# Late projection groups of a hybrid encoder layer: low weight parts from a copy in PSUM, token-major evictions through another ring

## The chip, the cores and the metric

The kernel runs on one core of a Trainium2 chip. The time is the device time of one execution in microseconds (us), the median of three runs. A separate execution was recorded by the hardware profiler, and all rows below come from that one. The engines are PE (TensorE), DVE (VectorE), ACT (ScalarE), POOL (GpSimd) and SP (SyncE, which here only issues DMAs). Each runs its own instruction stream strictly in the order in which it was built, and waits on semaphores.

## The reference

One layer on 512 tokens of width 2048. What matters here is the token mixing: one projection, whose columns feed four mixers.

```python
h = rms_norm(x, mix_pre_g) * (1.0 + sc_m) + sh_m
(a_q, a_k, a_v, a_gate, a_beta, a_alpha, b_q, b_k, b_v,
 c_q, c_k, c_v, d_u, d_v) = split(h @ w_in, offsets)
out_a = gated_deltanet(a_q, a_k, a_v, a_gate, a_beta, a_alpha, ...)   # conv, l2 norm, chunked delta rule
out_b = chunked_relbias_attention(b_q, b_k, b_v, rel_bias)            # 4 heads, softmax
out_c = swa_sink_attention(c_q, c_k, c_v, sinks, slopes)              # 4 heads, softmax
out_d = spatial_gating(d_u, d_v, sgu_norm_g, sgu_w, sgu_b)
y = concatenate([out_a, out_b, out_c, out_d]) @ w_out
x = x + gt_m * rms_norm(y, mix_post_g)
x = x + gt_f * rms_norm(conv_glu_ffn(...), ffn_post_g)                # the larger part of the time
```

The gates and shifts come from a matrix-vector product of `silu(c)` with `ada_w` (2048 x 12288), called the gemv below.

## The kernel before

Every large matmul is done in three passes on numbers split into a high and a low part (fp32r): `hi*hh + lo*hh + hi*hl`. A weight unit is a 128x1024 tile, loaded by one DMA into a ring `raw` (4 buffers) or, every second unit, into the ring `ada` (5), which the gemv's units use too. `wunit` cuts it into two halves of 128x512 and calls `split` for each. Without `shadow`, `split` writes `hi` on ACT and then `lo = raw - hi` on DVE. With `shadow`, ACT rounds the weights a second time into a PSUM tile `sh`, and DVE computes `lo = raw - sh` from that:

```python
        if shadow:
            sh = pp.tile([P, 512], F32R, tag=mtag(), name=nm("sh"), bufs=2)[:, :src.shape[1]]
            S.activation(sh, src, AF.Copy)
            S.activation(hi, src, AF.Copy)
            V.tensor_tensor(lo, src, sh, ALU.subtract)
            return
        S.activation(hi, src, AF.Copy)
        (eng or V).tensor_tensor(lo, src, hi, ALU.subtract)
```

PSUM holds two rings of 128x512 tiles. The ring `acc` (4 banks) holds the sums of the projections. The other (`mxa` and `mxb`, 2 banks each, taken in turn by `mtag()`) serves all tiles made by `mx(...)`: every matmul result of the DeltaNet, of the spatial gating and of the attentions. `sh` tiles come from that second ring. A ring hands its buffers out in the order in which the tiles stand in the program text: a tile gets its buffer when the tile that had it before has been read for the last time.

The input projection is done in groups. Early groups (step 0 to 5) run while the rows of `h` are being made. Late groups (`step is None`) are `bv`, `bk`, `ck`, `dv`, `bq`, `cq` and `du`: 52 weight units of 24 matmuls each, 1248 matmuls of 512 columns. `dv` and `bv` are token-major (`tm_group`), the rest feature-major (`fm_group`). Their results go through `ev_late_tm` (tiles `lt`) or `ev_late_fm` (`lf`) to DRAM. `between()` lets one to three background steps of the gemv in per unit (`RATE`).

In the program text the whole DeltaNet (lines 784 to 1046: convolutions and norms, decay matrices, a 32-step triangular solve on DVE at lines 944 and 946, and a recurrence of eight steps, lines 995 to 1046) comes first, then the groups `bv` to `dv`, the spatial gating, `bq`, the four heads of the `b` attention (lines 1096 to 1130), `cq`, `du`, the `c` attention (from line 1150) and the output projection. A scheduler then decides the order of each engine's stream: it may move an instruction ahead of others in the text as soon as its operands and its buffers are to be had.

Of the kernel before, what the change touches and what calls it, by code (L numbers as in the profile page):

```python
# [249 lines left out]
def trunk_kernel(ctx: ExitStack, tc: tile.TileContext, a: dict, out: bass.AP):  # L250
# [26 lines left out]
    def nm(s):  # L277
        uid[0] += 1
        return f"{s}{uid[0]}"

    def mt(s="m", shape=(P, 512), dt=F32):
        return cur[0].tile(list(shape), dt, tag="m", name=nm(s))

    def tt_(s="t"):
        return tp.tile([P, 512], F32, tag="t", name=nm(s))
# [4 lines left out]
    def acc(s="acc"):  # L290
        return pp.tile([P, 512], F32, tag="acc", name=nm(s))
# [56 lines left out]
    def wunit(src, nk, w, own=True, shadow=False):  # L348

        raw = wraw() if own else araw()  # L350
        nc.sync.dma_start(out=raw[:, :nk * w], in_=src[:, :nk * w])
        step = max(1, 512 // w)
        out_ = []
        for j in range(0, nk, step):
            m = min(step, nk - j) * w
            hi = wp.tile([P, 512], F32R, tag="hi", name=nm("hi"))
            lo = wp.tile([P, 512], F32R, tag="lo", name=nm("lo"))
            split(raw[:, j * w:j * w + m], hi[:, :m], lo[:, :m], None, shadow)
            out_ += [(hi[:, i * w:(i + 1) * w], lo[:, i * w:(i + 1) * w]) for i in range(min(step, nk - j))]
        return out_  # L360

    def wraw():
        return wp.tile([P, UW], F32, tag="raw", name=nm("raw"), bufs=NRAW)

    def araw():
        return gp.tile([P, UW], F32, tag="ada", name=nm("ada"), bufs=NADA)

    def split(src, hi, lo, eng=None, shadow=False):
# [10 lines that stand above are left out]
    def mm3(o, sh, sl, mh, ml, first, last):  # L379
        TE.matmul(o, sh, mh, start=first, stop=False)  # L380
        TE.matmul(o, sh, ml, start=False, stop=False)  # L381
        TE.matmul(o, sl, mh, start=False, stop=last)  # L382
# [156 lines left out]
    def between():  # L539
        pace[1] += pace[0]  # L540
        while pace[1] >= 1:
            pace[1] -= 1
            bg_step()

    def fm_group(g, evict, ws=None):
        _, keys, ks, step, us = g
        n = len(keys)
        if len(us) == 1:
            (ui, (uk, uc)) = us[0]
            if ws is None:  # L550
                ws = wunit(a["w_in"][ui], len(uk), len(uc), True, SH_IN and step > 0)
            for t in range(n):
                p_ = acc()
                o = slice(t * P, (t + 1) * P)
                for j, kt in enumerate(uk):
                    mm3(p_, ws[j][0][:, o], ws[j][1][:, o], hh[kt], hl[kt], j == 0, j == len(uk) - 1)
                evict(keys[t], p_, step)
            return
        ps = None
        for n_, (ui, (uk, uc)) in enumerate(us):  # L560
            ws = wunit(a["w_in"][ui], len(uk), len(uc), n_ % 2 == 0)
            between()
            if ps is None:
                ps = [acc() for t in range(n)]
            for j, kt in enumerate(uk):
                for t in range(n):
                    o = slice(t * P, (t + 1) * P)
                    mm3(ps[t], ws[j][0][:, o], ws[j][1][:, o], hh[kt], hl[kt], kt == ks[0], kt == ks[-1])
        for t in range(n):
            evict(keys[t], ps[t], step)  # L570

    def tm_mm(p_, sh, sl, wh, wl, first, last):
        TE.matmul(p_, sh, wh, start=first, stop=False)  # L573
        TE.matmul(p_, sh, wl, start=False, stop=False)  # L574
        TE.matmul(p_, sl, wh, start=False, stop=last)  # L575

    def tm_group(g, evict):
        _, key, ks, step, us = g
        ps = None
        for n_, (ui, (uk, uc)) in enumerate(us):  # L580
            w = len(uc)
            ws = wunit(a["w_in"][ui], len(uk), w, n_ % 2 == 0)
            between()
            if ps is None:
                ps = [acc() for _ in range(NTT)]
            order = [(j, tt) for j in range(len(uk)) for tt in range(NTT)]
            if len(us) == 1:
                order = [(j, tt) for tt in range(NTT) for j in range(len(uk))]
            for j, tt in order:
                kt = uk[j]  # L590
                sl = slice(tt * P, (tt + 1) * P)
                tm_mm(ps[tt][:, :w], hh[kt][:, sl], hl[kt][:, sl], ws[j][0], ws[j][1], kt == ks[0], kt == ks[-1])
        for tt in range(NTT):
            evict(key, tt, ps[tt], step)
# [62 lines left out]
    for s, ks in enumerate(KSTEPS):  # L657
        gs = [g for g in early if g[3] == s]
        fs = []
        upto = (KSTEPS[s + 1][-1] + 1) // 2 if s + 1 < len(KSTEPS) else 8  # L660
        while nextc < upto:
            fs += list(mod_units(nextc))
            nextc += 1
        for i, g in enumerate(gs):
            if s == 0 and i < 2:
                pass
            elif g[0] == "FM":
                fm_group(g, ev_early_fm)
            else:
                tm_group(g, ev_early_tm)  # L670
            n = -(-len(fs) // max(1, len(gs) - 2 - i)) if s else FS0[i]
            for f in fs[:n]:
                f()
            fs = fs[n:]
# [19 lines left out]
    def rtile(s, dt=F32):  # L694
        if mixing_open[0]:
            return gp.tile([P, 512], dt, tag="xn", name=nm(s), bufs=NBR)
        return mt(s, dt=dt)
# [62 lines left out]
        nc.sync.dma_start(out=std[STG[n_] + j], in_=t)  # L760

    def ev_late_tm(key, tt, ps, step):
        t = tt_("lt")
        S.activation(t, ps, AF.Gelu_apprx_tanh if key == "dv" else AF.Copy)  # L764
        nc.sync.dma_start(out=std[STG[key] + tt], in_=t)

    def late_groups(name, rate):
        pace[0] = rate
        for g in late:
            if (g[1][0][0] if g[0] == "FM" else g[1]) == name:  # L770
                if g[0] == "FM":
                    fm_group(g, ev_late_fm)
                else:
                    tm_group(g, ev_late_tm)

    def staged(name, j):
        t = mt("sd")
        nc.sync.dma_start(out=t, in_=std[STG[name] + j])
        return t
# [83 lines left out]
    for tt in range(NTT):  # L863
# [4 lines left out]
        t = mt("kp")  # L868
# [4 lines left out]
    for tt in range(NTT):  # L873
# [3 lines left out]
        t = mt("vt")  # L877
# [196 lines left out]
    for tt in range(NTT):  # L1074
        t = staged("dv", tt)
# [5 lines left out]
    for tt in range(NTT):  # L1081
        t = tmt[("dv", tt)]
        V.tensor_scalar(t, t, mv[:, tt, 0:1], vr[:, tt:tt + 1], ALU.subtract, ALU.mult)
        V.tensor_tensor(t, t, sgg, ALU.mult)
    for g in range(4):
# [4 lines left out]
        t = cur[0].tile([P, 512], F32, tag="sgo", name=nm("sgo"), bufs=4)  # L1090
# [7 lines left out]
    for h in range(H):  # L1098
# [5 lines left out]
        for i in range(NTT):  # L1104
            w = P * (i + 1)
# [11 lines left out]
        for j in range(NTT):  # L1117
# [3 lines left out]
            t = mt("pt")  # L1121
# [19 lines left out]
    for h in range(H):  # L1141
# [4 lines left out]
        for i in range(NTT):  # L1146
            w = P if i == 0 else 2 * P
# [15 lines left out]
        for i0 in (0, 2):  # L1163
            ps = mx("cT")
            for i in (i0, i0 + 1):
                w = P if i == 0 else 2 * P
# [3 lines left out]
            t = mt("ct")  # L1170
# [58 lines left out]
    for cb in range(4):  # L1229
# [3 lines left out]
        ws = {}  # L1233
# [186 lines left out]
    def draw():  # L1420
        n = nraw[0] % (NRAW + NRAW1 + NRAW2)
        nraw[0] += 1
        if NRAW1 <= n < NRAW + NRAW1:
            return wraw()
        if n < NRAW1:
            return ap_[0].tile([P, UW], F32, tag="raw1", name=nm("raw"), bufs=NRAW1)
        return dn[0].tile([P, UW], F32, tag="raw2", name=nm("raw"), bufs=NRAW2)
# [176 lines left out]
    ws, acts = {}, {}  # L1604
# [15 lines left out]
    for c in (0, 2):  # L1620
        t = draw()
        nc.sync.dma_start(out=t, in_=gtd[c:c + 2, :].rearrange("c n -> (c n)").partition_broadcast(P))
        gts.append(t)
    for tt in range(NTT):
# [3 lines left out]
        for h in range(2):  # L1628
            t = draw()
# [58 lines left out]
```

## Time and profile before

| | us |
|---|---|
| median of 3 runs (lowest to highest) | 2328.01 (2320.36 to 2335.2) |
| the profiled execution | 2326.28 |
| its span in the trace | 2324.4 |
| busy PE, DVE, ACT, POOL | 2192.7, 1698.5, 1460.2, 1074.6 |

The span is what the trace covers from the first to the last instruction; some 2 us lie outside it. A busy engine is one with an instruction under way; matmuls overlap in the array, so PE's busy time says little of its rate, and the distance from one start to the next is what to read. The groups below give single instructions (start, duration), groups of instructions, and stretches of the span.

### The profile page before, as it was taken

Reading aid. Unit: us, or ns where it says so; the run is one execution under the profiler, and the core shown is the slowest. Engines: PE = TensorE matmul, PEld = TensorE weight load, DVE = VectorE, ACT = ScalarE, POOL = GpSimd, SP = SyncE. Lnnn points to the kernel's source line nnn. Section 1 sums busy time; section 2 is a strip of 40 time slices with the busy share of each in tenths; the row PEclk is TensorE's granted clock in tenths of the full one; section 3 lists DMA queues with packets and bytes.
Section 4 is the critical chain, followed back from the end, with each engine's and each line's share of the span. In section 5 each row is a group of like instructions: output and inputs, shape, how many; then the busy total and the mean of one; then the engine's idle time right before and its main releaser. Section 6 shows DMA issues by size and latency. Waiting matters only on the chain. (4 is left out here: it accounts for less than half of the span.)

```text
span 2324.4 us, 31330 instructions
## 1 busy us (share of the span) xinstructions
PE 2192.7 (94%) x9852; PEld 1735.8 (75%) x9852; DVE 1698.5 (73%) x2665; ACT 1460.2 (63%) x2636; POOL 1074.6 (46%) x848
## 2 busy tenths in 40 slices
PE   5999999999999999989999999999999999999998
PEld 3878776777677786777788887777777777777776
DVE  5887678976878745966665668788788866767777
ACT  5776465354567544666677677776776777666663
POOL 4563022242323200356546365765665675574643
PEclk8999999999999899999999999999999999999999
DMA  8876455676888745678853557456545634425333
GB/s 298 287 264 232 163 190 173 221 229 238 294 286 295 252 152 166 217 262 289 279 211 132 179 175 270 165 191 210 197 171 206 224 133 166 161 100 198 119 124 144
DMA packets 206574, 480.24 MB, mean 207 GB/s; under 512 B 32692, under 2 KB 74180, under 8 KB 206408
## 3 DMA queue, kind: packets, MB, share of 16 engines
q1 hardware_dynamic: 199576, 477.19, 58.8%
q10 hardware_dynamic: 6832, 1.06, 0.3%
q8 instruction: 78, 1.28, 0.2%
q14 instruction: 88, 0.72, 0.1%
HBM read 399.50 MB, written 78.67 MB: 206 GB/s over the span
## 5 line engine op out<-in xcount | busy, mean ns | idle before, releaser
L1480 PE MATMUL X<-hi,ah 128*128 128x512 f32 x960 | 386.1, 402 | 21.5 <-DVE c L1492 9.0
L435 POOL TENSOR_TENSOR ga<-ga,ada 128x512 f32<-128x512 f32 (+1 forms) x167 | 228.4, 1368 | 372.5 <-ACT ada L434 351.7
L1482 PE MATMUL X<-hi,al 128*128 128x512 f32 x960 | 383.6, 400 | 1.9 <-DVE al L1417 1.9
L1481 PE MATMUL X<-lo,ah 128*128 128x512 f32 x960 | 383.3, 399 | 0.0
L1446 DVE TENSOR_TENSOR lo<-raw,hi 128x512 fp32r<-128x512 f32 x360 | 269.2, 779 | 103.6 <-ACT hi L1445 103.2
L1467 POOL TENSOR_TENSOR raw<-raw 128x512 f32<-128x512 f32 x120 | 162.8, 1359 | 326.7 <-ACT hi L1442 243.6
L1480 PE MATMUL Z<-hi,ah 128*128 128x512 f32 x720 | 286.1, 397 | 9.4 <-ACT c L1490 5.5
L1443 DVE TENSOR_TENSOR lo<-raw,sh 128x512 fp32r<-128x512 f32 x360 | 240.6, 683 | 71.2 <-ACT sh L1441 30.9
L1441 ACT ACTIVATE sh<-raw 128x512 fp32r<-128x512 f32 x360 | 210.6, 588 | 128.1 <-DMA raw<-w_dn 62.8
L1482 PE MATMUL Z<-hi,al 128*128 128x512 f32 x720 | 285.1, 396 | 0.0
L1481 PE MATMUL Z<-lo,ah 128*128 128x512 f32 x720 | 284.8, 396 | 0.0
L1445 ACT ACTIVATE hi<-raw 128x512 fp32r<-128x512 f32 x360 | 214.0, 625 | 92.7 <-PE X L1482 30.7
L1442 ACT ACTIVATE hi<-raw 128x512 fp32r<-128x512 f32 x360 | 221.5, 622 | 35.4 <-PE Z L1482 25.0
L1480 PEld LDWEIGHTS X<-hi,ah 128*128 128x128 f32 x960 | 182.8, 190 | 69.1 <-DVE c L1492 10.3
L380 PE MATMUL acc<-hh,hi 128*128 128x512 f32 x544 | 221.7, 411 | 9.1 <-ACT lt L764 6.6
L382 PE MATMUL acc<-hh,lo 128*128 128x512 f32 x544 | 221.3, 410 | 4.2 <-DVE lo L374 4.2
L381 PE MATMUL acc<-hl,hi 128*128 128x512 f32 x544 | 223.0, 410 | 0.4 <-POOL hl L493 0.4
L1482 PEld LDWEIGHTS X<-hi,al 128*128 128x128 f32 x960 | 182.7, 190 | 44.8 <-DVE al L1417 2.3
L1481 PEld LDWEIGHTS X<-lo,ah 128*128 128x128 f32 x960 | 182.6, 190 | 42.1 <-DVE lo L1443 0.6
L377 DVE TENSOR_TENSOR lo<-raw,hi 128x512 fp32r<-128x512 f32 (+1 forms) x162 | 121.2, 761 | 67.2 <-ACT hi L376 65.9
L1480 PEld LDWEIGHTS Z<-hi,ah 128*128 128x128 f32 x720 | 135.4, 188 | 44.5 <-ACT c L1490 6.8
L432 DVE SCALAR_TENSOR_TENSOR ga<-ada,cond,ga 128x512 f32<-128x512 f32 (+1 forms) x183 | 150.5, 822 | 18.1 <-DMA ada<-ada 16.0
(363 smaller groups left out, 4684.6 us busy)
## 6 DMA issues: line engine op xcount, KB each, us to landing
ada<-ada SPq DMA_DIRECT2D x184, 512.0 KB, 4.6
raw<-w_up SPq DMA_DIRECT2D x172, 512.0 KB, 5.9
raw<-w_dn SPq DMA_DIRECT2D x86, 512.0 KB, 5.9
raw<-w_in SPq DMA_DIRECT2D x56, 512.0 KB, 4.3
partd<-c SPq DMA_DIRECT2D x80, 256.0 KB, 4.0
c<-partd SPq DMA_DIRECT2D x80, 256.0 KB, 3.9
actd<-q SPq DMA_DIRECT2D x40, 512.0 KB, 3.3
ar<-actd SPq DMA_DIRECT2D x35, 512.0 KB, 3.5
```

The source lines that it names most:

```text
L380: TE.matmul(o, sh, mh, start=first, stop=False)
L381: TE.matmul(o, sh, ml, start=False, stop=False)
L382: TE.matmul(o, sl, mh, start=False, stop=last)
L435: G.tensor_tensor(accs[eng], accs[eng], src, ALU.add)
L1441: S.activation(sh, src, AF.Copy)
L1442: S.activation(h_, src, AF.Copy)
L1443: V.tensor_tensor(l_, src, sh, ALU.subtract)
L1445: S.activation(h_, src, AF.Copy)
L1446: eng.tensor_tensor(l_, src, h_, ALU.subtract)
L1480: TE.matmul(ps, ah[:, sl], wh, start=st_, stop=False, skip_group_check=True)
L1481: TE.matmul(ps, ah[:, sl], wl, start=False, stop=False, skip_group_check=True)
L1482: TE.matmul(ps, al[:, sl], wh, start=False, stop=sp_, skip_group_check=True)
```

## The change

Late groups call `wunit` with `shadow` set (early groups of the same code keep it off, since their `step` is a number), and the tiles `lt` come from the ring `xn` of five tiles instead of the ring `t` of three.

```diff
@@ fm_group, tm_group
-            ws = wunit(a["w_in"][ui], len(uk), len(uc), n_ % 2 == 0)
+            ws = wunit(a["w_in"][ui], len(uk), len(uc), n_ % 2 == 0, step is None)
...
-            ws = wunit(a["w_in"][ui], len(uk), w, n_ % 2 == 0)
+            ws = wunit(a["w_in"][ui], len(uk), w, n_ % 2 == 0, step is None)
@@ ev_late_tm
-        t = tt_("lt")
+        t = rtile("lt")
```

Where the first late matmuls stand on PE. `acc` are sums of the late group `bv` (lines 573 to 575), `g` and `nB` belong to the DeltaNet's gates and norms. Before:

```order
L575 MATMUL acc_3472<-hi_3506,hl_498 128x512
L822 MATMUL g_2542<-la_2509,cst 128x16
L823 MATMUL g_2542<-la_2509,cst 128x16
L824 MATMUL g_2542<-la_2509,cst 128x16
L825 MATMUL g_2542<-la_2509,cst 128x16
L852 MATMUL nB_2583<-sq_2572,ones 128x512
L573 MATMUL acc_3473<-hi_3506,hh_495 128x512
L574 MATMUL acc_3473<-lo_3507,hh_495 128x512
```

Now:

```order
L573 MATMUL acc_3479<-hi_3458,hh_238 128x512
L822 MATMUL g_2542<-la_2509,cst 128x16
L823 MATMUL g_2542<-la_2509,cst 128x16
L824 MATMUL g_2542<-la_2509,cst 128x16
L825 MATMUL g_2542<-la_2509,cst 128x16
L852 MATMUL nB_2583<-sq_2572,ones 128x512
L846 MATMUL ss_2596<-ones,sq_2594 128x1 x4
L852 MATMUL nB_2605<-sq_2594,ones 128x512
```

Ahead of `g` there stood 39 late matmuls and now stand 4 (the first of each sum, which need only `hi`); behind `nB` 34 more followed before the next norm, and now none.

One step of the recurrence on PE: `pm` from the state `S`, `pm` from `u`, `ps` (the state's update) from `vp`. Before:

```order
L1006 MATMUL pm_3271<-S_3177,kq_2561 128x128
L382 MATMUL acc_4955<-hh_1437,lo_5036 128x512
L380 MATMUL acc_4954<-hh_1710,hi_5081 128x512
L381 MATMUL acc_4954<-hl_1713,hi_5081 128x512
L382 MATMUL acc_4954<-hh_1710,lo_5082 128x512
L1016 MATMUL pm_3280<-u_3272,mtb_3078 64x128 x2
L1016 MATMUL pm_3280<-u_3272,mtb_3127 64x128 x2
L380 MATMUL acc_4955<-hh_1710,hi_5081 128x512
L381 MATMUL acc_4955<-hl_1713,hi_5081 128x512
L382 MATMUL acc_4955<-hh_1710,lo_5082 128x512
L380 MATMUL acc_4954<-hh_1717,hi_5081 128x512
L1023 MATMUL ps_3287<-vp_3285,kp_2755 128x128 x4
```

Now:

```order
L1006 MATMUL pm_3271<-S_3177,kq_2561 128x128
L1016 MATMUL pm_3280<-u_3272,mtb_3078 64x128 x2
L1016 MATMUL pm_3280<-u_3272,mtb_3127 64x128 x2
L1023 MATMUL ps_3287<-vp_3285,kp_2755 128x128 x4
L1030 MATMUL pm_3271<-vp_3285,at_2870 64x128 x2
```

No late matmul stands inside the step. From `g` to the end of the last step there are none at all on PE now; 1232 of the 1248 stand behind it, the next twelve between the last `pm` and the last transpose `oT`. On DVE and POOL the gemv's steps of that stretch have moved behind it too.

The `b` attention on PE, from one head's scores `sc` to its transposed weights `pT`. Before, at the second head:

```order
L1107 MATMUL sc_5260<-sd_5220,sd_5222 128x512
L380 MATMUL acc_5895<-hh_238,hi_5874 128x512
L381 MATMUL acc_5895<-hl_241,hi_5874 128x512
L382 MATMUL acc_5895<-hh_238,lo_5875 128x512
L380 MATMUL acc_5894<-hh_329,hi_5874 128x512
L381 MATMUL acc_5894<-hl_332,hi_5874 128x512
L382 MATMUL acc_5894<-hh_329,lo_5875 128x512
L380 MATMUL acc_5895<-hh_329,hi_5874 128x512
L1120 MATMUL pT_5271<-cst,p_5229 128x128
```

Now, at the first head:

```order
L1107 MATMUL sc_5323<-sd_5283,sd_5285 128x512
L380 MATMUL acc_5640<-hh_238,hi_5613 128x512
L381 MATMUL acc_5640<-hl_241,hi_5613 128x512
L380 MATMUL acc_5641<-hh_238,hi_5613 128x512
L381 MATMUL acc_5641<-hl_241,hi_5613 128x512
L1120 MATMUL pT_5334<-cst,p_5292 128x128
```

These four are the only late matmuls inside the four heads (before, 188 stood between the first head's `sc` and the last head's `pv`); `cq` follows behind them. In the same way four, and no more, stand ahead of the spatial gating's matmuls, between `dv` and `bq`. From the first matmul of the `c` attention on, PE's order is much as it was.

## Rows read from the trace of the kernel before

**Rows 1.** Stretches: PE, PEld, DVE, ACT, POOL busy (instructions), PEclk, DMA share, GB/s.

```profile
264.00:376.00 112.00, 106.96 (x489) 82.67 (x490) 85.85 (x161) 67.53 (x101) 28.93 (x22) 1.00 0.51 170
376.00:420.00 44.00, 39.56 (x260) 28.44 (x258) 40.11 (x67) 17.48 (x31) 10.52 (x7) 0.96 0.63 195
420.00:486.00 66.00, 59.37 (x243) 47.29 (x242) 62.91 (x102) 26.28 (x43) 24.30 (x15) 0.92 0.67 236
486.00:508.00 22.00, 22.00 (x184) 18.03 (x183) 9.78 (x14) 14.98 (x31) 5.34 (x7) 1.00 0.79 225
508.00:578.00 70.00, 67.53 (x385) 52.46 (x382) 49.83 (x67) 31.88 (x54) 25.00 (x18) 0.93 0.69 245
...
606.00:680.00 74.00, 68.31 (x295) 49.11 (x295) 58.75 (x111) 46.55 (x97) 25.98 (x22) 1.00 0.79 285
680.00:694.00 14.00, 14.00 (x62) 11.30 (x62) 7.84 (x12) 6.75 (x12) 2.92 (x2) 1.00 0.90 306
```

**Rows 2.** PE in order of time, first and last of 36 consecutive late matmuls.

```profile
440.62 0.39 PE L575 MATMUL acc<-hi,hl 128*128 128x512 f32 x1
...
448.78 0.40 PE L574 MATMUL acc<-lo,hh 128*128 128x512 f32 x1
```

**Rows 3.** DVE groups from 264 to 590 us: busy, mean ns; idle before.

```profile
L432 DVE SCALAR_TENSOR_TENSOR ga<-ada,cond,ga 128x512 f32<-128x512 f32 x59 | 50.3, 853 | 4.3 <-DMA ada<-ada 3.9
L377 DVE TENSOR_TENSOR lo<-ada,hi 128x512 fp32r<-128x512 f32 x41 | 33.6, 821 | 19.3 <-ACT hi L376 17.9 <-PE acc L381 1.1 <-PE acc L382 0.2
...
L946 DVE TENSOR_TENSOR x<-x,tmpi 128x496 f32<-128x496 f32 (+30 forms) x31 | 19.1, 615 | 0.5
L944 DVE TENSOR_TENSOR tmpi<-kts,x 128x496 f32<-128x496 f32 (+30 forms) x31 | 18.0, 582 | 0.3
```

**Rows 4.** Instructions of line 374 in the early groups: min/median/max ns.

```profile
L374 DVE TENSOR_TENSOR lo<-raw,sh x56: 674/681/690, 63.0 to 245.4; 128x512 fp32r<-128x512 f32 x56
```

**Rows 5.** One head of the norms on DVE, in order of time.

```profile
290.07 0.76 DVE L856 TENSOR_TENSOR kq<-cv,nB 128x256 f32<-128x256 f32 x2 [2.40 <-PE nB L852]
...
296.67 0.69 DVE L792 SCALAR_TENSOR_TENSOR cv<-pa,cv 128x512 f32<-128x512 f32 x1
...
303.13 0.75 DVE L856 TENSOR_TENSOR kq<-cv,nB 128x256 f32<-128x256 f32 x2 [2.40 <-PE nB L852]
```

**Rows 6.** Solve on DVE, in order of time.

```profile
420.39 0.67 DVE L944 TENSOR_TENSOR tmpi<-kts,x 128x496 f32<-128x496 f32 x1
...
436.12 1.57 DVE L946 TENSOR_TENSOR x<-x,tmpi 128x416 f32<-128x416 f32 x1
...
484.70 0.17 DVE L946 TENSOR_TENSOR x<-x,tmpi 128x16 f32<-128x16 f32 x1
```

**Rows 7.** Recurrence, in order of time.

```profile
545.38 1.08 PE L1016 MATMUL pm<-u,mtb 64*64 64x128 f32 x8
...
549.62 1.16 PE L1006 MATMUL pm<-S,kq 128*128 128x128 f32 x8
...
552.11 1.08 PE L1016 MATMUL pm<-u,mtb 64*64 64x128 f32 x8
```

**Rows 8.** DMA issues from 264 to 694 us: KB each, median us to landing.

```profile
sd<-std SPq DMA_DIRECT2D x19, 256.0 KB, 5.4
...
std<-lt SPq DMA_DIRECT2D x8, 256.0 KB, 4.0
```

**Rows 9.** First head of the `b` attention, in order of time.

```profile
606.10 0.49 PE L1107 MATMUL sc<-sd,sd 128*128 128x128 f32 x2
...
620.14 2.32 PE L1126 MATMUL pv<-pt,sd 128*128 128x512 f32 x8
```

**Rows 10.** Waits from 264 to 700 us: total, times, longest.

```profile
PE acc L380 <- ACT lt L764: 6.6, 1, 6.6
```

**Rows 11.** A stretch of 5 us, columns as in rows 1.

```profile
465.00:470.00 5.00, 0.00 (x0) 0.00 (x0) 4.96 (x10) 3.75 (x6) 2.85 (x2) 0.60 0.55 176
```

**Rows 12.** Recurrence, at another point in time.

```profile
566.07 2.08 PE L1023 MATMUL ps<-vp,kp 64*128 64x128 f32 x8
```

## The prediction

> **What bounds the kernel now.** I looked first at the stretches of the span in which late groups run [rows 1]. From 264 to 694 us PE is busy for 90 to 100% of every stretch, while ACT and POOL are far from full. Busy time is no rate, so the next view is PE in order of time: 36 late matmuls in a row start from 440.62 to 448.78 us, which is 0.2331 us from start to start [rows 2]. The 1248 late matmuls are therefore 1248 x 0.2331 = 291 us of PE at its best pace. The stretch has 430 us. The other 139 us are PE's own work for the DeltaNet, the spatial gating and the `b` attention, with few gaps. So this part of the kernel is bound by PE, and only because late matmuls fill PE while the DeltaNet's long chains on DVE, ACT, POOL and DMA go on. The DeltaNet takes 314 of these 430 us (264 to 578), and DVE does much of its work there for others: 59 gemv steps of 853 ns and 41 `lo` of 821 ns for the units in `ada` [rows 3], and as many again for those in `raw`.
>
> **The change, part by part.**
>
> *A rounding into PSUM.* 104 halves get one more ACT instruction, of about the length of its other copies, some 0.6 us: 62 us more on an engine that was busy for about half of these stretches [rows 1]. On DVE a `lo` from `sh` takes 681 ns and never over 690 [rows 4], one from `hi` in SBUF 821 on average for the `ada` half [rows 3]; that is some 8 us less DVE for the 104. Neither is on the path when PE is the bound. I cost both at nothing. If the cover went, the ACT part would be at worst 62 us.
>
> *Where the copies live.* `sh` takes its bank from the ring that the DeltaNet's tiles use, and the ring hands banks out in the order of the text. All DeltaNet tiles stand ahead of the first late `sh`. Before, a late unit needed only `raw`, `hi`, `lo` and `acc`, so it could run beside the DeltaNet. Now its `lo` waits until the last DeltaNet tiles are read, and the order of the streams shows it: 16 late matmuls ahead of the last transpose `oT`, 1232 behind. Four matmuls stand ahead of the spatial gating's and four inside the `b` attention. PE's streams are in order, so this is no matter of luck at run time. The gemv's steps go with the units (their tiles share `ada`). So a stretch in which two things ran beside each other becomes one thing after the other, and its length is a sum.
>
> *The DeltaNet alone.* Its time falls, because foreign work leaves DVE and PE. I go by stretches [rows 1].
> - Norms and convolutions, 112 us. One head takes 303.13 - 290.07 = 13.1 us [rows 5]. Its second half, from the end of line 792 (297.36) to the next `kq`, is 5.8 us of a chain over ACT, PE, DVE and POOL without foreign work, and stays. The first 7.3 us hold two `lo` and two gemv steps, 2.7 us. So 10.4 us a head, a factor of 0.8: 90 us.
> - Decay matrices and their way through DRAM, 44 us. Gemv steps and the `ada` half of `lo` hold DVE for (50.3 + 33.6) / 326 = 26% of the time [rows 3], 11 us here, and some POOL contention goes: 32 us. The DMA round trip in it does not shrink.
> - The solve, 66 us. 62 dependent instructions from 0.67 us down to 0.17 [rows 6], mean 0.42, with about 0.04 between them: 28 us. As they ran they were busy for 19.1 + 18.0 = 37 us [rows 3], since some take 1.57 us at 416 columns, where a longer one of 496 columns takes 0.67 [rows 6]. These long instructions I take to be POOL's doing: the gemv's adds on POOL run in this stretch (24.30 us busy [rows 1]), and they move away. [...]
> - The product of inverses, 22 us, mostly DMA and small products: 21.
> - The recurrence, 70 us. One step at the full clock took 552.11 - 545.38 = 6.7 us with eight late matmuls inside [rows 7], mostly under waits: 6.2 alone. Eight steps are 50 us, and the four transposes `oT`, which stand ahead of the next step's matmul on PE and wait for a norm over ACT and DVE, cost about 2 us each: 58.
>
> Together 90 + 32 + 28 + 21 + 58 = 229 us. The floor would be DVE's own part: 248 us busy in 264 to 578 [rows 1] less 50 + 34 [rows 3] and another 34 for the units in `raw`, is about 130. [...]
>
> *The late matmuls.* 1232 x 0.2331 = 287 us.
>
> *The spatial gating*, which had late matmuls beside it, now stands bare between `dv` and `bq`. `lt` must land in DRAM (4.0 us) and come back as `sd` (5.4 us) [rows 8], around that four evictions, the layer norm on DVE and the small products: 20 us, between 14 and 26.
>
> *The `b` attention.* The first head took from 606.10 to the end of `pv` at 622.46, 16.4 us [rows 9], with gemv steps and `lo` in its chain; bare I take 14 a head. The ring of four banks keeps heads apart (four in 74 us before [rows 1]). Four heads: 56 us, between 46 and 70.
>
> *The larger ring for `lt`.* The fourth eviction of `dv` waited for an earlier one's DMA, and PE stood for 6.6 us [rows 10]. That wait goes. But in the same place the bare spatial gating now makes PE wait for 20 us, which hold these 6.6, so I count nothing. Nobody else uses the ring `xn` at that time.
>
> *Starting again.* Where PE had stood still, from 465 to 470 us, its clock was 0.60 on average [rows 11]. It will stand still three times and then start at the lower of its two levels, and the denser gemv may hold it here and there: 12 us, between 3 and 35.
>
> *The sum.* After: 264 + 229 + 287 + 20 + 56 + 12 = 868 us where the `c` attention began at 694 before. That is 174 us more. From there on PE's order is as it was, as is the gemv's progress, so nothing comes back. Against the profiled execution of 2326.3 us: **2500 us**. That execution lies 2 us under the median, which I leave aside.
>
> **Rivals.**
>
> [...]
>
> *DMA holds the late groups.* In the last 24 units there are three background steps each, eight in nine of which load 0.52 MB, as does the unit: (24 + 64) x 0.524 = 46 MB. At 285 to 306 GB/s, the most seen in a longer stretch [rows 1], that takes 150 to 162 us against 576 x 0.2331 = 134 on PE. About 24 us more: 2525 us. For it: the rows at 606 to 694. Against: part of these steps falls into the `b` attention.
>
> *A faster DeltaNet.* If its chains overlap better than one head after the other, it comes nearer to DVE's floor: 165 in place of 229 us, 2436 us.
>
> *The other side: not slower.* For that the late matmuls would have to start among the DeltaNet's steps after all, with `sh` tiles slipping into banks as they come free; then only the 6.6 us of `lt` and the slow restart behind it would be gained: about 2317 us. It decides itself at how many late matmuls stand ahead of the last step; it would take some 700, and the order has four before the last step begins.
>
> **How the numbers follow.** Forecast 0.68, half clock 0.12, DMA 0.12, faster DeltaNet 0.06, not slower 0.02. The bounds of the terms give 264 + 205 + 287 + 14 + 46 + 3 = 819 us (2451) and 264 + 262 + 293 + 26 + 70 + 35 = 950 us (2582); 205 takes each DeltaNet stretch a tenth shorter. The range, 2450 to 2575, holds the forecast and the two slower rivals. About 1% is what a measurement of this kernel can tell from no change: faster 0.01, within it 0.01, slower 0.98.
>
> **What would show it.** In the changed kernel's trace PE should be mostly idle from about 265 to 490 us, with DMA and POOL near zero from about 280 on; lines 944 and 946 should have no instruction over 0.7 us and span some 28 us; late matmuls should follow at 0.233 us; two gaps, of about 20 and 56 us, before and after `bq`; and the first `c` score near 868 us. The prediction is wrong if late matmuls stand in the DeltaNet, if the DeltaNet alone is not between 205 and 262 us, or if the first `c` score to the end is not as long as before.

## The result, and the profile after

The changed kernel takes 2592.94 us in the median (4 runs, 2589.99 to 2609.71) against 2329.82 (4 runs, 2320.36 to 2335.2): 1.1147 times as long, with a 95% interval of 1.1118 to 1.1175. I had forecast 2500 and a range up to 2575. The direction and the mechanism came out as forecast, the size did not: 263 us were lost, not 174.

Stretches of the changed kernel, with the columns of [rows 1]. I cut them at the events at which I had cut the kernel before: the first line 887 less 2 us, the first and the last line 944/946, the last `px` plus 3.6 us, the last `pm`; then the gating, `bq`, the `b` attention, and `cq` with `du` up to the first `c` score.

```profile
264.00:359.20 95.20, 39.88 (x127) 24.79 (x125) 50.20 (x116) 34.45 (x46) 8.72 (x8) 0.54 0.03 9
359.20:395.60 36.40, 18.08 (x148) 10.04 (x148) 22.95 (x48) 6.97 (x12) 0.00 (x0) 0.69 0.14 30
395.60:425.30 29.70, 0.00 (x0) 0.00 (x0) 26.92 (x63) 0.00 (x0) 0.00 (x0) 0.50 0.01 1
425.30:448.00 22.70, 11.73 (x123) 11.44 (x124) 0.69 (x1) 7.81 (x18) 2.10 (x4) 0.50 0.27 46
448.00:528.50 80.50, 63.02 (x260) 52.07 (x258) 21.90 (x35) 14.14 (x24) 0.00 (x0) 0.50 0.08 23
528.50:708.30 179.80, 163.45 (x673) 129.47 (x672) 76.34 (x102) 91.08 (x160) 46.10 (x35) 0.95 0.62 215
708.30:741.70 33.40, 8.85 (x37) 7.49 (x37) 19.61 (x33) 14.60 (x24) 10.02 (x8) 0.59 0.80 268
741.70:785.80 44.10, 44.10 (x188) 35.49 (x189) 25.69 (x32) 24.77 (x43) 14.52 (x12) 1.00 0.82 292
785.80:859.00 73.20, 44.08 (x110) 24.80 (x108) 34.39 (x81) 30.83 (x73) 15.88 (x15) 0.67 0.50 166
859.00:948.00 89.00, 89.00 (x382) 71.59 (x381) 48.51 (x65) 55.66 (x100) 27.46 (x20) 1.00 0.80 272
```

The first five rows are the bare DeltaNet: POOL is nearly idle, DMA is busy for at most 0.27 of a row, and PE has 0.50 to 0.69 of its clock. The sixth holds the late groups up to `dv`. The eighth (`bq`) and the tenth (`cq`, `du`) are late matmuls alone, with PE busy throughout at a clock of 1.00. The seventh and the ninth are the two bare gaps that the order of the streams had shown, one on each side of `bq`. Against the terms of the sum:

| term | forecast, us | measured, us | how measured |
|---|---|---|---|
| norms and convolutions | 90 | 95.2 | row 1 |
| decay matrices | 32 | 36.4 | row 2 |
| solve | 28 | 29.7 | row 3 |
| product of inverses | 21 | 22.7 | row 4 |
| recurrence | 58 | 80.5 | row 5 |
| 1232 late matmuls | 287 | 287 | same pitch, below |
| spatial gating | 20 | 31.3 | 33.4 less four late matmuls (2.1) |
| `b` attention | 56 | 71.6 | 785.82 to 858.93, less four late matmuls (1.5) |
| stops of PE on evictions | 0 | 13.9 | waits of PE at 582.21 (5.0) and 662.06 (7.9), and 1.0 on a `lo` at 650.15 |
| starting again, and the last `oT` | 12 | 15.7 | what is left of 684.0 (264.0 to 948.0) |
| from the first `c` score to the end | 0 | 12.2 | 2591.0 - 948.0 against 2324.4 - 693.6 |

The differences add up to 92 us. The solve (first and last of lines 944 and 946, to compare with [rows 6]) is what I had said, and no instruction in it is over 0.68 us:

```profile
395.63 0.68 DVE L944 TENSOR_TENSOR tmpi<-kts,x 128x496 f32<-128x496 f32 x1 [4.25 <-DMA x<-x]
...
423.88 0.18 DVE L946 TENSOR_TENSOR x<-x,tmpi 128x16 f32<-128x16 f32 x1
```

PE in order of time: first and last of a run of late matmuls, to compare with [rows 2], and below them two steps of the recurrence, which came earlier:

```profile
538.56 0.40 PE L573 MATMUL acc<-hi,hh 128*128 128x512 f32 x1
...
559.56 0.40 PE L573 MATMUL acc<-hi,hh 128*128 128x512 f32 x1
```

```profile
495.50 2.07 PE L1023 MATMUL ps<-vp,kp 64*128 64x128 f32 x8 [0.68 <-ACT vp L1018]
...
504.89 2.07 PE L1023 MATMUL ps<-vp,kp 64*128 64x128 f32 x8 [0.68 <-ACT vp L1018]
...
509.54 2.08 PE L1006 MATMUL pm<-S,kq 128*128 128x128 f32 x8 [0.68 <-ACT o L1032]
...
513.66 1.12 PE L1044 MATMUL oT<-cst,o 128*128 128x128 f32 x4 [2.05 <-DVE o L1041]
...
517.35 2.07 PE L1023 MATMUL ps<-vp,kp 64*128 64x128 f32 x8 [0.68 <-ACT vp L1018]
```

The late run holds 91 matmuls, so the pitch is 21.00 / 90 = 0.2333 us: where late matmuls follow each other, the added rounding and the PSUM source cost PE nothing. In the recurrence `pm` and `ps` take 1.96 to 2.08 us in every step, where [rows 7] had 1.08 to 1.16. That is the length of the long one of [rows 12], and the granted clock was 0.50 (row 5). Of the 1450 stretches of 0.2 us from 300 to 590 us 1082 are at 0.50, 358 at 1.00 and 10 between; in the kernel before 118, 1326 and 6. So these traces show two levels. At the lower one, behind the stop of [rows 10], the first late matmuls of the kernel before (470.62 to 474.89 us, at 0.50) start 0.427 us apart.

What PE waited for from 535 to 948 us (total, times, longest), to compare with [rows 10]:

```profile
PE pT L1120 <- DVE p L1063: 15.6, 12, 4.1
PE sg L1088 <- issue: 15.3, 1, 15.3
PE sc L1107 <- DMA sd<-std: 13.4, 3, 5.6
PE acc L380 <- ACT lt L764: 12.0, 2, 7.0
PE acc L573 <- ACT lf L759: 7.9, 1, 7.9
```

The first three belong to the bare gating and heads. The other two are stops in front of an eviction, which I had not in the sum. ACT's own order ahead of the one of 7.0 us, in front of the gating:

```profile
710.95 0.72 ACT L430 ACTIVATE ga<-ada,cond 128x512 f32<-128x512 f32 x1 [4.04 <-DMA ada<-ada]
711.58 0.71 ACT L434 ACTIVATE ada<-ada,cond 128x512 f32<-128x512 f32 x1
712.19 1.13 ACT L373 ACTIVATE hi<-ada 128x512 fp32r<-128x512 f32 x2
713.34 1.28 ACT L764 ACT_TABLE_LOAD   x1
714.63 2.06 ACT L764 ACTIVATE lt<-acc 128x512 f32<-128x512 f32 x4
```

The sums in `acc` were complete at 708.26, but the evictions stand on ACT behind a gemv scaling that waits for its weights (4.04 us), a second scaling, two `hi` copies and a table load. The stop of 5.0 us, in front of the `lt` at 581.56, comes by way of DVE and the new banks (DVE first, then ACT):

```profile
573.51 1.54 DVE L432 SCALAR_TENSOR_TENSOR ga<-ada,cond,ga 128x512 f32<-128x512 f32 x2 [6.94 <-DMA ada<-ada]
...
575.68 0.60 ACT L372 ACTIVATE sh<-raw 128x512 fp32r<-128x512 f32 x1 [4.82 <-DVE lo L374]
```

A gemv step stands on DVE ahead of a `lo` and waits 6.94 us for its weights; that `lo` has to read its `sh` before the bank is free for ACT's next `sh`, and ACT, held there for 4.82 us, comes late to the eviction.

### The profile page after: what moved, and what is told of

It reads as the page before. It is cut to its first block, busy times and chain, and to the rows that moved or that the text cites. A ratio compares the mean times of both kernels' runs of the same rounds, so it can differ in the third digit from the quotient of the medians.

```text
span 2591.0 us, 31479 instructions
## 1 busy us (share of the span) xinstructions
PE 2271.3 (88%) x9852; PEld 1790.3 (69%) x9852; DVE 1674.4 (65%) x2665; ACT 1513.6 (58%) x2739; POOL 1067.0 (41%) x848
## 5 line engine op out<-in xcount | busy, mean ns | idle before, releaser
L435 POOL TENSOR_TENSOR ga<-ga,ada 128x512 f32<-128x512 f32 (+1 forms) x167 | 219.6, 1315 | 556.6 <-ACT ada L434 512.7
L1443 DVE TENSOR_TENSOR lo<-raw,sh 128x512 fp32r<-128x512 f32 x360 | 240.1, 683 | 71.6 <-ACT sh L1441 38.8
L432 DVE SCALAR_TENSOR_TENSOR ga<-ada,cond,ga 128x512 f32<-128x512 f32 (+1 forms) x183 | 158.0, 863 | 123.3 <-DMA ada<-ada 120.5
L434 ACT ACTIVATE ada<-ada,cond 128x512 f32<-128x512 f32 (+1 forms) x167 | 113.4, 706 | 96.7 <-DMA ada<-ada 88.3
```

The costliest lines, as they stand in the source:

```text
L435: G.tensor_tensor(accs[eng], accs[eng], src, ALU.add)
L1443: V.tensor_tensor(l_, src, sh, ALU.subtract)
```

## The experiments

Each ratio is to runs of the kernel before that were made beside it (their medians were 2326.6 to 2330.0 us).

| kernel | median, us | ratio to before, 95% interval |
|---|---|---|
| e_lt | 2330.54 | 1.0022 [1.0008, 1.0036] |
| e_shadow | 2598.95 | 1.1186 [1.1166, 1.1207] |
| e_sbuf | 2332.9 | 1.0042 [1.0008, 1.0077] |
| e_claim | 2599.88 | 1.1178 [1.1153, 1.1203] |
| e_tail | 2407.92 | 1.035 [1.0323, 1.0376] |
| e_inter | 2432.61 | 1.046 [1.0429, 1.0491] |
| e_interp | 2324.54 | 0.9989 [0.9972, 1.0007] |
| e_raw | 2625.17 | 1.1278 [1.1246, 1.131] |
| e_rawb | 2345.26 | 1.0081 [1.0058, 1.0104] |
| e_ballast | 2579.81 | 1.1086 [1.1052, 1.112] |
| e_balb | 2604.5 | 1.1192 [1.1156, 1.1228] |
| e_pref | 2582.22 | 1.1088 [1.1069, 1.1106] |

### Is it the bank, the rounding or the other ring?

**e_lt** and **e_shadow** are the two halves of the change.

```diff
 e_lt: the kernel before with
-        t = tt_("lt")
+        t = rtile("lt")
 e_shadow: the changed kernel with
-        t = rtile("lt")
+        t = tt_("lt")
```

> The kernel before with one edit: the token-major late evictions take their tiles from the ring of five row tiles; no late low part goes through PSUM. Bank order (the theory: late units wait because their PSUM copies stand behind all DeltaNet tiles in the ring): 754 late matmuls still stand beside the DeltaNet, so the time is that of before, less the 6.6 us of one wait if that is on the path: 2315 to 2332 us. Rival, eviction ring (the row-tile ring is what holds the late groups back): over 2400 us.

> The change without the eviction ring: late low parts through PSUM, evictions in the ring of three. Bank order: as the changed kernel, 2585 to 2610 us, first c score near 948 us. Rival, eviction ring: most of the loss gone, under 2450 us.

Both times lie in their forecasts (the first `c` score of e_shadow came at 959 us, not near 948). The whole loss is in the PSUM half. The eviction ring alone gains nothing, and the stop of 6.6 us [rows 10], which I had said goes, is still there. The wait of PE in e_lt:

```profile
PE acc L380 <- ACT lt L764: 8.3, 1, 8.3
```

In the kernel before, ACT reached the first `lt` of `dv` late in the same way:

```profile
466.22 1.33 ACT L434 ACTIVATE ada<-ada,cond 128x512 f32<-128x512 f32 x2 [2.90 <-DMA ada<-ada]
...
469.38 1.58 ACT L764 ACTIVATE lt<-acc 128x512 f32<-128x512 f32 x3
```

Between the two stand a `hi` copy and the table load. PE had stopped at 463.4 us and went on at 470.03, right behind the first of these three evictions; PE did not wait for the fourth, at 475.78. The one wait for an earlier eviction's DMA (3.43 us, at 322.88) was in `bv`, and did not stop PE.

**e_sbuf** keeps both roundings of late weights but puts the first into `lo` itself, in SBUF. **e_claim** keeps the bank and drops nearly all of the rounding.

```diff
 e_sbuf, late units
-            sh = pp.tile([P, 512], F32R, tag=mtag(), name=nm("sh"), bufs=2)[:, :src.shape[1]]
-            S.activation(sh, src, AF.Copy)
+            S.activation(lo, src, AF.Copy)
             S.activation(hi, src, AF.Copy)
-            V.tensor_tensor(lo, src, sh, ALU.subtract)
+            V.tensor_tensor(lo, src, lo, ALU.subtract)
 e_claim, late units
-            S.activation(sh, src, AF.Copy)
+            S.activation(sh[:, 0:2], src[:, 0:2], AF.Copy)
             S.activation(hi, src, AF.Copy)
-            V.tensor_tensor(lo, src, sh, ALU.subtract)
+            V.tensor_tensor(lo[:, 0:2], src[:, 0:2], sh[:, 0:2], ALU.subtract)
+            V.tensor_tensor(lo[:, 2:], src[:, 2:], hi[:, 2:], ALU.subtract)
```

> The changed kernel, but the second rounding of late weights goes into the lo tile itself in SBUF, and DVE subtracts in place: the same two ACT roundings and the same wait of DVE for the first of them, without a PSUM bank. Bank order: 744 late matmuls stand beside the DeltaNet again, so 2315 to 2345 us. Rival, rounding cost (62 us more of ACT, standing ahead of hi in its stream, is what slows the late groups): 2380 us and more, with late matmuls further apart than 0.2331 us.

> The changed kernel, but ACT rounds only two columns of each late half into the PSUM tile (about 0.2 us in place of 0.6) and DVE takes the other 510 from hi in SBUF: the bank is claimed in the same order, nearly without the added rounding. Bank order: 2560 to 2605 us, the late groups behind the DeltaNet as in the changed kernel. Rival, rounding cost: under 2450 us.

Both forecasts hold. The rounding without the bank costs 0.4% (0.1 to 0.8%), and the bank nearly without the rounding (0.17 us a half in place of 0.59) costs everything. The two together leave no room for ACT's added work as the cause.

### Does the order in which the banks are claimed do it?

**e_inter** keeps every late rounding in PSUM but writes the late units into the text of the DeltaNet, the gating and the heads of `b`, one or two at a time. **e_interp** is the same text without the bank (`lo = raw - hi`).

```diff
 e_inter, for instance in the norms, the solve and the recurrence
+            late_to(lcnt[0] + 1)
             y = conv_silu2((key, h), base + h)
...
+        if j % 4 == 0:
+            late_to(lcnt[0] + 1)
...
+        if n:
+            late_to(min(36, lcnt[0] + 1))
         pm2 = mx("pm2")
 e_interp: as e_inter, and
-            ws = wunit(..., n_ % 2 == 0, step is None)
+            ws = wunit(..., n_ % 2 == 0, False)
```

> The changed kernel with the text of the late units cut up and written between the pieces of the DeltaNet, the spatial gating and the heads of b, one or two units at a time; every late unit is still rounded into PSUM. By the order 864 late matmuls stand beside the DeltaNet. Bank order: the banks now come in an order in which both can go on, so the loss is gone: 2310 to 2375 us. Rival, sharing (the late groups and the DeltaNet get in each other's way in four banks, whatever the order): over 2450 us.

> The kernel of e_inter (text of the late units written between the pieces of the DeltaNet, the gating and the heads of b, larger eviction ring), but with the low parts taken from hi in SBUF as in the kernel before. e_inter lost 105 us against before although 864 late matmuls stood beside the DeltaNet. Sharing (four banks for DeltaNet tiles and sh tiles make each wait for the other): without the bank claims the loss is gone, 2315 to 2350 us. Rival, the text (the cut itself puts late work in bad places): it stays over 2400 us.

e_inter hit neither of its two forecasts. Some 157 of the 263 us come back when the claims are written where the work is meant to be, which is the order of the banks; 106 us stay. e_interp shows that these are not the text's doing: without the claims the same text is as fast as before. So in this order of claims, too, four banks for two customers cost something; whether another order would cost nothing was not tried. The stretch of the recurrence in e_inter, up to the last `oT` (columns as above):

```profile
546.00:652.00 106.00, 88.28 (x447) 68.42 (x446) 52.25 (x76) 45.50 (x79) 29.09 (x20) 0.81 0.55 185
```

It is 76 us in the kernel before (508 to 584). At the last `oT` e_inter is 68 us behind, at the first `c` score 106. How much of that is waits for a bank and how much is that claims and reads come out in a tighter order, the profile doesn't say: of waits of ACT for an `sh` bank it names 20.5 us in 264 to 800. That stays open.

**e_tail** rounds only `cq` and `du` into PSUM (`tm_group` calls `wunit` as before the change), so that the DeltaNet is covered again and only the gating and the `b` attention are bare.

```diff
-            ws = wunit(a["w_in"][ui], len(uk), len(uc), n_ % 2 == 0, step is None)
+            ws = wunit(a["w_in"][ui], len(uk), len(uc), n_ % 2 == 0, step is None and keys[0][0] in ("cq", "du"))
```

> The changed kernel with the PSUM rounding in the last two late groups alone (cq and du); the other five are split as before. 829 late matmuls stand beside the DeltaNet again, but none beside the spatial gating and the b attention, and 380 behind it. Sum of bare stages: the DeltaNet as before, the gating and the b attention bare as in the changed kernel (30 and 73 us), so the first c score near 755 us and about 2395 us in all. Rival, only the DeltaNet counts: within 1% of before, 2310 to 2350 us.

It is 2408, 13 us over the sum, with the first `c` score at 763.8 us where I had 755. The sum of bare stages holds here too, to within these 9 us: from the last `oT` to the first `b` score it takes 26 us, the four heads 64 (610.4 to 675), `cq` and `du` behind them 89. The rival falls.

### Why were the bare stages longer than I said?

**e_ballast** gives the recurrence eight idle matmuls a step back.

```diff
+        S.activation(jb[r], bal[r, 0:1], AF.Copy, scale=v_[r, 0:1])   # once a step: holds the next eight back
...
+        for j in range(8):
+            TE.matmul(bal, hh[j][:, 0:P], hh[j], start=True, stop=True)
         for h in range(H):
             TE.matmul(pm2[ro, h * P:(h + 1) * P], ...)
```

> The changed kernel with eight idle matmuls of 512 columns a step in the recurrence, into a bank that nobody uses (their result is dropped), as many as there were late ones before, and one small ACT copy a step that keeps them in their step. Half clock (the bare recurrence took 88 us, where I had 58, because PE's clock stayed at its lower level): clock over 0.9 in the recurrence, which takes 55 to 68 us, and 2565 to 2580 us in all. Rival, bare chain (the recurrence is long for its waits on DVE and ACT): 88 to 105 us and 2593 to 2610 us.

Stretches of e_ballast, the last one the whole stage, then PE's state updates in order of time:

```profile
450.00:460.00 10.00, 9.32 (x42) 7.55 (x40) 2.07 (x3) 1.44 (x3) 0.00 (x0) 0.65 0.04 10
...
480.00:490.00 10.00, 7.99 (x53) 6.48 (x54) 4.10 (x8) 2.77 (x7) 0.00 (x0) 1.00 0.12 33
490.00:500.00 10.00, 9.32 (x51) 7.69 (x52) 2.73 (x4) 2.03 (x4) 0.00 (x0) 0.83 0.07 21
...
444.70:515.20 70.50, 61.80 (x317) 49.69 (x315) 21.91 (x35) 16.20 (x32) 0.00 (x0) 0.77 0.09 27
```

```profile
480.20 1.16 PE L1038 MATMUL ps<-vp,kp 64*128 64x128 f32 x8 [0.68 <-ACT vp L1030]
...
488.79 1.16 PE L1038 MATMUL ps<-vp,kp 64*128 64x128 f32 x8 [0.68 <-ACT vp L1030]
...
497.19 1.16 PE L1038 MATMUL ps<-vp,kp 64*128 64x128 f32 x8 [0.68 <-ACT vp L1030]
```

More work made the stage shorter: 70.5 us from the same event to the same event, where it was 80.5. (The 88 us of the forecast ran on to the last `oT`; counted so, e_ballast takes 77.) The granted clock rose to 0.65 from 450 us on, was 1.00 from 480 to 490 and 0.83 in the next 10 us; over the whole stage it was 0.77. From 480 us on `ps` takes 1.16 us, as the kernel before has it at a clock of 1.00, where the changed kernel had 2.07. A step with an `oT` then takes 8.6 us (480.20 to 488.79) where the changed kernel took 12.5 (504.89 to 517.35), one without 8.4 (488.79 to 497.19) where it took 9.4 (495.50 to 504.89), and that with eight idle matmuls in each (1.9 us at 0.233 us a matmul). The bare chain as the only cause falls, and the lower clock is shown to be a cause. Not shown is that it is the whole: 10 of the 22.5 us came back, and what the idle matmuls themselves hold up was not separated. My clock of over 0.9 and my 55 to 68 us were missed on either count, and the time (2579.8) lies at the upper end of its range.

**e_raw** takes the gemv out of the late units' way: all late units use `raw`, and the gemv has `ada` for itself. **e_rawb** does the same to the kernel before.

```diff
-            ws = wunit(..., n_ % 2 == 0, step is None)
+            ws = wunit(..., step is None or n_ % 2 == 0, step is None)
```

> The changed kernel, but all late weight units use the ring raw, so that the gemv's units have the ring ada for themselves; by the order 58 gemv steps of DVE then stand ahead of the solve and none between the last DeltaNet state and the spatial gating. Gemv crowding (theory: evictions stand on ACT behind gemv scalings that wait for their DMA, four stops of 5 to 8 us, and SP's loads for the gating and the heads stand behind the gemv's): the stops on lt and lf go, the gating is under 28 us and the b attention under 66 us, 25 to 45 us less there; the DeltaNet gets back part of that as foreign DVE and POOL work, up to 25 us: 2545 to 2590 us. Rival, the stops have another cause: they stay, over 2590 us.

> The kernel before, but with all late weight units in the ring raw, so that the gemv has ada to itself; by the order 42 gemv steps of DVE stand ahead of the solve in place of 19. In e_raw that took the stops on evictions away (42 us in the late groups) and cost 95 us in the bare DeltaNet. Here PE is the bound beside the DeltaNet. If PE's stream hides the denser gemv: 2300 to 2322 us. If the gemv's DVE and POOL work lengthens the DeltaNet beyond what late matmuls can fill: 2335 to 2400 us.

The first half of e_raw's forecast came out. No wait on `lt` or `lf` is left up to the first `c` score, the gating takes 16.7 us and the heads 64, and the late groups in all (last `oT` to first `c` score) 371 us in place of 413. The second half was four times too small: the last `oT` comes 96 us later, where I had up to 25. Stretches of e_raw: norms, solve, gating, heads:

```profile
289.00:396.00 107.00, 35.03 (x96) 21.28 (x96) 91.27 (x115) 56.21 (x82) 65.04 (x45) 0.50 0.64 224
467.00:519.00 52.00, 0.00 (x0) 0.00 (x0) 49.05 (x79) 11.39 (x18) 20.72 (x14) 0.50 0.58 194
788.20:804.90 16.70, 6.45 (x34) 6.19 (x33) 11.24 (x24) 4.76 (x9) 0.00 (x0) 0.69 0.74 259
849.00:913.00 64.00, 42.18 (x111) 23.84 (x110) 23.66 (x67) 22.50 (x60) 0.44 (x3) 0.71 0.18 60
```

The gemv now crowds into the norms, where DVE is busy for 91 of 107 us, and into the solve, which takes 52 us where it took 29.7 (and 66 in the kernel before). The last `oT` comes at 630 us in place of 534. What the late groups win, the bare DeltaNet loses twice over. In the kernel before the same move costs 0.8% (0.6 to 1.0), the second of e_rawb's two forecasts: PE's stream doesn't hide it there either.

**e_pref** loads the next head's tiles of `b` ahead of this head's end.

```diff
             pr.append(p_)
+            if i == 1 and h + 1 < H:
+                nxt = head_loads(h + 1)     # bk, bq, tb and its memset, which stood at the loop's top
```

> The changed kernel, but the loads for the next head of b (its two staged tiles and its bias) are written in the text after the second score row of the head before, so that they no longer stand on SP behind that head's result. Loads between heads (three waits of PE on them, 5.6, 3.9 and 3.9 us): they go, the four heads take 58 to 63 us where they took 73, and 2578 to 2586 us in all. Rival, the loads are late for the gemv's transfers in the same queue: the heads stay at 70 us or more and the time at 2588 to 2600 us.

SP in the changed kernel, at the end of the first head, and PE of e_pref at the same place:

```profile
805.70 0.33 SPq L1058 DMA_DIRECT2D mixd<-ob  x1
806.08 0.92 SPq L778 DMA_DIRECT2D sd<-std  x2
```

```profile
800.17 4.63 PE L1133 MATMUL pv<-pt,sd 128*128 128x512 f32 x8
804.60 1.88 PE L1112 MATMUL sc<-sd,sd 128*128 128x128 f32 x6
```

In the changed kernel the loads stand on SP behind the result of the head before, which ends it, and PE's next `sc` came at 810.62. In e_pref it starts before `pv` has drained. The three waits are gone, the heads take 62 us, and the time is 11 us less, as forecast.

**e_balb** gives the `b` attention idle matmuls, as e_ballast did the recurrence.

```diff
+            S.activation(jb, bal[:, 0:1], AF.Copy, scale=den)
             softmax_norm(p_, w, den)
             pr.append(p_)
+            ballast(5)
```

> The changed kernel with five idle matmuls of 512 columns behind each of the 16 score rows of the b attention (result dropped), and one small ACT copy each that keeps them there. The b attention took 73 us, where I had 56; PE's clock was 0.70 there. Half clock: clock over 0.85 and 56 to 66 us for the four heads, 2578 to 2588 us in all. Rival, the chain of loads and softmax: 73 us or more, 2590 to 2615 us.

The clock rose (e_balb first, then the changed kernel):

```profile
816.00:836.00 20.00, 14.03 (x49) 9.07 (x49) 8.37 (x21) 8.44 (x22) 5.33 (x6) 0.84 0.42 152
```

```profile
805.00:825.00 20.00, 11.16 (x27) 6.26 (x26) 9.28 (x20) 7.68 (x18) 5.89 (x5) 0.66 0.47 167
```

but the heads took 78.8 us (789.05 to 867.82), with a clock of 0.85 over them. The 80 idle matmuls are 18.6 us at 0.233 us a matmul, and the loads between heads were still late (3.9 to 5.3 us each). So here the lower clock is not what sets the time, or the cure costs as much as it gives; the run doesn't separate the two.

## Why the prediction was wrong in size

The mechanism came out; what failed is the price of the bare stages in the sum. Of the 92 us that it lacked, the recurrence has 22.5, the `b` attention 15.6, the stops on evictions 13.9 and the part behind the first `c` score 12.2 (both at nothing in the sum), the gating 11.3, and five smaller terms 16.7. The recurrence is the largest, and alone more than the 18 us between the top of the range and the measured time. The terms are added up from the upper bounds to 950 us, and the first `c` score came at 948.0; but the range stopped at 2575, under the 2582 of these bounds, and they left the part behind that score unchanged. No run shows the 262 us that these bounds have for the DeltaNet: the changed kernel took 264.5 us, 80.5 of them in the recurrence at a clock of 0.50. Two of my own signs of being wrong came: the bare DeltaNet took 264.5 us, not 205 to 262, and the part behind the first `c` score was 12.2 us longer.

*What bounds the kernel, and what the ring does.* Right, and shown: e_sbuf and e_claim separate the bank from the rounding, e_inter and e_interp the order of the claims from the text. The late groups went behind the DeltaNet and gave up their cover, and the time is a sum of stages.

*The DeltaNet alone.* Four of its five stages are within 6 us of the forecast. The recurrence is the step that failed, 80.5 us for 58. "6.2 alone" was worked out from rows at the full clock (1.00 from 543 to 553 us), and from a step without an `oT`. PE's state updates of the kernel before show both kinds, together with the row at 566.07 of [rows 12]:

```profile
547.52 1.16 PE L1023 MATMUL ps<-vp,kp 64*128 64x128 f32 x8
...
554.25 1.16 PE L1023 MATMUL ps<-vp,kp 64*128 64x128 f32 x8
```

The first distance, without an `oT`, is 6.7 us, the second, with one, 11.8, though with late matmuls inside: 5.1 more, where I had added 2. I gave half clock a chance of only 0.12: that a PE busy for over half of each step keeps its clock was my estimate, and the run shows the opposite. PE was busy for 63 of 80.5 us, with no gap over 2.2 us, and yet the clock was 0.50 throughout. A step has four products at some 2 us where they take 1.05 to 1.16 at a clock of 1.00 in the kernel before, which would be up to 29 us over the eight steps if all stood on the chain; the measured surplus is 22.5 us, and 5 us in the norms, at a clock of 0.54. In the norms I had called the second half of a head free of foreign work; two `lo` stand there in the kernel before, at 297.27 and 298.97 us.

*The larger ring.* "That wait goes" was wrong: e_lt. I had read the wait for an earlier eviction's DMA into `dv`, where PE stopped; it was in `bv`. What held the evictions of `dv` was ACT's order, not the ring.

*The gemv.* I saw that its steps move with the units, and drew no price from it. Denser among the late groups, it put steps that wait for DMA ahead of evictions, on ACT itself or on DVE ahead of the `lo` that frees a bank (13.9 us, and 7.0 inside the gating), and its loads ahead of the gating's. e_raw takes these away, and the gating falls from 33.4 to 16.7 us. ACT's added rounding is not what held the evictions: in e_claim, nearly without it, the three stops are there, 22.5 us in all. The 12.2 us in the `c` attention and behind it stay open in part. PE stood 7.1 us there on an `lf`, in front of which ACT had waited 3.59 and 2.80 us for the gemv's weights. With the gemv moved ahead that part takes 1623 us in e_raw in place of 1643, but 1615 in e_rawb in place of 1631, so 8 us between the two kernels remain without it.

*The `b` attention.* "Bare I take 14 a head" was right for three heads (13.3 to 14.0 us from `sc` to the end of `pv`); the first, beside the gemv, took 19.2. What lacked was 13.4 us of loads between the heads, which lay beside late matmuls before: e_pref.

*DMA as the bound.* The rival falls: `cq` and `du` ran at 0.233 us a matmul with DMA at 0.80. *A faster DeltaNet* (it took 264.5 us, not 165) and *not slower* fall too.

## What to carry to other kernels

A tile from a shared ring is a place in a queue. Before giving an operation such a tile, look at who stands ahead of it in the text and whether the operation was meant to run beside them. When cover goes, price each bare stage as it will run, with its loads issued late (13.4 us of waits between the heads here) and PE at the lower clock (0.50 in the recurrence, 0.67 in the heads), not from rows in which PE was kept full by the very work that leaves. Where background work moves, ask which in-order queue it will stand in front of.

## What I had not expected of the hardware

In 448 to 528.5 us PE was busy for 63 us with gaps of at most 2.2 us, at 0.50 of its clock throughout; with eight more matmuls of 512 columns a step the granted clock rose to 0.65 and then to between 0.83 and 1.00, and 10 us were gained by adding work.

In the solve of the changed kernel, where POOL is silent, no DVE instruction is over 0.68 us. In e_raw, where the gemv runs beside it and no matmul does, some take up to 1.68. Stretches of that solve, and DVE's instructions in two of them:

```profile
467.30:472.00 4.70, 0.00 (x0) 0.00 (x0) 3.94 (x6) 1.45 (x4) 0.00 (x0) 0.50 0.96 306
472.10:476.60 4.50, 0.00 (x0) 0.00 (x0) 4.12 (x3) 1.84 (x3) 4.21 (x3) 0.50 0.14 52
513.30:515.80 2.50, 0.00 (x0) 0.00 (x0) 2.47 (x2) 0.41 (x1) 2.42 (x2) 0.50 0.00 0
```

```profile
470.10 0.64 DVE L944 TENSOR_TENSOR tmpi<-kts,x 128x464 f32<-128x464 f32 x1
...
473.81 1.68 DVE L944 TENSOR_TENSOR tmpi<-kts,x 128x448 f32<-128x448 f32 x1
```

With DMA at 0.96 and POOL idle, DVE runs at the changed kernel's pace (0.64 us at 464 columns in both); with POOL at work it is slow there (1.68 us at 448 columns, in the changed kernel 0.62), with DMA at 0.14 and at 0.00. Of the 62 instructions of the solve 11 are long, in e_raw as in the kernel before (0.9 to 1.1 us longer than the same ones in the changed kernel), and each of them runs beside one of the gemv's adds on POOL; none that ran clear of such an add is long. So the long ones belong to the adds, as the prediction took it, and not to the gemv's transfers.
